# Eight floats of padding in front of the large SBUF tile of a hybrid decoder trunk

## The chip, the cores and the metric

The kernel runs on one core of one Trainium2 chip. The time is device microseconds of one execution, the median of several runs. The profile is one further execution, recorded by the hardware profiler; its times are given from the first instruction to the last (the span).

## What is computed

The reference is a decoder of four layers over 256 tokens of 1024 numbers, all in float32. Each layer is a token mixer (HGRN2, FoX attention, Mamba-2 SSD, HGRN2) followed by a PEER feed-forward part, and a final RMS norm ends it. The PEER part is what moves the data:

```python
def peer_ffn(h, w_q, sub_keys, u_tab, v_tab):
    ...
        q = (xb @ w_q).reshape(M, PEER_HEADS, 2, PEER_HALF)
        s = jnp.einsum('mhcd,hckd->mhck', q, sub_keys).astype(jnp.float32)
        sv, si = lax.top_k(s, PEER_TOPK)
        ...
        u = jnp.take(u_tab, idx, axis=0)
        v = jnp.take(v_tab, idx, axis=0)
        act = jax.nn.gelu(jnp.einsum('md,mhkd->mhk', xb, u).astype(jnp.float32), approximate=False) * gates
        return jnp.einsum('mhk,mhkd->md', act.astype(xb.dtype), v)
```

For each token, 8 heads choose 16 of 16384 experts each. Every chosen expert needs its own row of u and of v, 1024 floats each, which differ from token to token. That is 256 x 8 x 16 = 32768 row pairs for each layer, 8192 bytes a pair.

## The kernel before

**The eight stages.** A stage is one layer's PEER part for one half of the tokens. The halves are 128 tokens, but a gather serves 64 tokens twice over: 128 partitions hold two experts for each of 64 tokens. A stage is 64 pairs of gathers (8 heads by 8 positions q, and in each pair g = 0 and 1, the two groups of 64 tokens), so 512 pairs, 1024 gathers in all. The last pair is split into six smaller gathers, which makes 1028.

**One gather.** u and v stand side by side in one table, in_uv, with rows of 2048 floats. `gather` (line 1517) is an indirect DMA on POOL's queue: each of the 128 partitions gets one row of 8192 bytes, 1 MB for a gather. `fetches` issues them as long as the deque `ring` has a free buffer. The ring holds GB, seven buffers of 2 x 1024 floats for each partition, and now and then a spot that is free for a while.

**What is done with it.** `dot` multiplies the u half by the token's vector and sums it on VectorE (line 230 is the helper that all VectorE work goes through). `active` applies GELU on ScalarE and scales a 128x64 matrix dg with it (helper line 243). `spread` multiplies dg with the v half on TensorE into an accumulator (line 1587) and gives the buffer back to the ring.

**The work beside it.** While stage s runs, the mixer, the norms and the queries of stage s + 1 run piece by piece between the pairs; a cost estimate decides when the next piece is let in. Their weights come as units of 128 x 2048 floats, 1 MB, issued by `loads` (line 417) in a list's order, into one of these places: a raw buffer (pool raw, two of them), a kept spot (eight, plus one in mix), a home borrowed from another part of the arena. SP issues most of them; ScalarE (ACT) issues those that fill a kept spot in step with the projections, on a queue of its own. A few query units are parked as two halves in free columns of mix (line 415). The places come from PARK:

```python
PARK = {"hg": (6 * D, 7 * D), "fox": (6208, 7232), "ssd": (192, 192 + 3 * D + 96)}
```

**Where things lie.** The pool c has buffers of its own in the order in which its tiles are asked for: cst (784 floats for each partition), par (386), fst (192), the arena (49216), and then small tiles (eps, spare, rts, trimask, m64). Behind that pool lie the two raw buffers and the pool wk2 with dg, dots and the routing's small tiles. A tile's size is rounded up to 32 bytes. Below the pool lie 2048 bytes for each partition that hold DMA descriptors (SCRATCH), and four constants of 32 bytes each. So the arena begins at byte 2048 + 128 + 3136 + 1568 + 768 = 7648 of each partition, the first raw buffer at 205024. cst begins at 2176, par at 5312 and fst at 6880. The four dots buffers lie 32 bytes apart.

The arena is one tile that is cut by hand: h, xT, XR, keys, SS, mix, kept, gb. All these widths are multiples of 64 floats, so that every part starts as far past a multiple of 256 bytes as the arena does. Within mix, all places for loads do too, except the second of the SSD layer's parked halves at float 3360, which is 52 x 256 + 128 bytes into mix.

The change stands in `trunk`, which is the whole program; the lines that it moves stand below it by one.

Of the kernel before, what the change touches and what calls it, by code (L numbers as in the profile page):

```python
# [11 lines left out]
F32 = mybir.dt.float32  # L12
# [7 lines left out]
P = 128  # L20
# [170 lines left out]
def trunk(ctx: ExitStack, tc: tile.TileContext, d: dict, out: bass.AP):  # L191
    nc = tc.nc
    SB = bass.MemoryType.PSUM
    cpool = ctx.enter_context(tc.tile_pool(name="c", bufs=1))
# [11 lines left out]
    fst = cpool.tile([P, P + 8 * 2 * DEPTH], F32, name="fst")  # L206
    sizes = (("h", D), ("xT", D), ("XR", 2 * D), ("keys", UNIT), ("SS", 2048), ("mix", MIX), ("kept", NKEPT * UNIT),
             ("gb", NGB * 2 * D))
    arena = cpool.tile([P, sum(n for _, n in sizes)], F32, name="arena")
    at_, o_ = {}, 0  # L210
    for name, n in sizes:
# [1555 lines left out]
```

## Time and profile before

| | |
|---|---|
| time, median of 3 runs | 3123.55 us (3118.79 to 3123.78) |
| profiled execution: time, span | 3126.04 us, 3124.2 us |
| mean granted TensorE clock | 0.946 |
| moved by DMA | 1266.72 MB, mean 405 GB/s over the span |
| busy: TensorE, VectorE, ScalarE, POOL | 83%, 67%, 50%, 39% |

In the profile's rows, L230 is line 230 of the kernel, out<-in names the tiles that an instruction writes and reads, and x1028 counts instructions. The DMA section lists the queues with their packets, megabytes, and the time that the packets took as a share of 16 DMA engines over the span or the stretch asked for. A packet here is one contiguous piece for one partition, or a semaphore word of 4 bytes that reports an engine's part of a DMA as done. Shares can exceed 100% slightly, where packets overlap. With a stretch given, the same section tells of that stretch alone, and that is how the price of packets of one kind can be read.

A row of the table of stretches has the stretch, its length, the busy time of TensorE, weight loads, VectorE, ScalarE and POOL with the number of instructions, and at its end the granted clock, the DMA share and GB/s. A row of waits reads: who waited, for whom, us in total, times, longest.

### The profile page before, as it was taken

The page shows a single profiled execution, that of the slowest core. Times are in us where ns is not written, and L with a number is a line of the kernel's source. Part 1 is how long each engine was busy: PE and PEld are TensorE (multiplying, and loading weights), DVE is VectorE, ACT ScalarE, POOL GpSimd, SP SyncE. Part 2 cuts the span into 40 slices and gives each one's busy share as a digit, 9 for nine tenths or more (in the row PEclk, how much of TensorE's full clock was granted, in tenths as well). Part 3 has the DMA queues.
Part 4 walks back from the last instruction along what each step waited for, and adds up shares of the span by engine and source line. Part 5 has one row for each costly group of instructions (what it writes and reads, how often), then busy time and mean ns, then how long its engine had stood idle before and what let it go on. Part 6 is the DMA issues. An engine that isn't in the chain of part 4 may idle for free.

```text
span 3124.2 us, 34210 instructions
## 1 busy us (share of the span) xinstructions
PE 2595.8 (83%) x10106; PEld 1102.8 (35%) x10106; DVE 2103.1 (67%) x5583; ACT 1566.2 (50%) x4486; POOL 1230.2 (39%) x1036
## 2 busy tenths in 40 slices
PE   9899887887689996988878998878877899876666
PEld 4444342233234452333234542523322343521111
DVE  1677667665857767778476886677657677677754
ACT  3465434463445744577345784355444565443433
POOL 0234334443443444333343333343334443455454
PEclk9999989998999998999999999999989999999999
DMA  8799999999999999999998999999999999999998
GB/s 338 281 410 420 420 419 419 408 412 420 418 412 419 397 419 411 401 416 404 407 416 357 391 412 420 418 411 418 420 416 409 401 418 420 419 419 420 419 420 341
DMA packets 176184, 1266.72 MB, mean 405 GB/s; under 512 B 19585, under 2 KB 20225, under 8 KB 22913
## 3 DMA queue, kind: packets, MB, share of 16 engines
q0 software_dynamic: 147776, 1073.81, 83.8%
q1 hardware_dynamic: 24480, 163.47, 12.7%
q10 hardware_dynamic: 3744, 27.26, 2.1%
q8 instruction: 83, 1.36, 0.2%
q14 instruction: 101, 0.82, 0.1%
HBM read 1263.41 MB, written 1.05 MB: 405 GB/s over the span
## 4 chain that ended last, share of the span: by engine, by line
DMA 48%; PE 16%; issue 14%; DVE 13%; POOL 5%; ACT 4%; POOLq 0%; DVEq 0%; ACTq 0%
DMA arena<-in_uv,ix 46%; DVE arena L230 9%; PE pj L271 6%; PE acc L1587 5%; POOL arena L1517 5%; PE ps L271 4%; ACT L243 2%; DVE eq L230 1%; DMA raw<-in_ssm 1%; ACT dg L243 1%; PE ps L275 1%; ACT arena L243 1%; DVE af L230 1%; DVE gs L230 0%; DVE si L230 0%
## 5 line engine op out<-in xcount | busy, mean ns | idle before, releaser
L1517 POOL DMA_INDIRECT arena<-in_uv,ix x1028 | 1227.8, 1194 | 1877.8 <-PE acc L1587 1095.9
L230 DVE SCALAR_TENSOR_TENSOR arena<-arena 128x1024 f32<-128x1024 f32 (+2 forms) x1088 | 1266.1, 1172 | 815.8 <-DMA arena<-in_uv,ix 797.5
L1587 PE MATMUL acc<-arena,dg 128*64 128x512 f32 x4096 | 1396.9, 660 | 472.4 <-ACT dg L243 468.4
L243 ACT ACTIVATE dots<-dots 128x1 f32<-128x1 f32 x1024 | 203.1, 198 | 1239.6 <-DVE arena L230 1237.8
L1587 PEld LDWEIGHTS acc<-arena,dg 128*64 128x64 f32 x4096 | 344.0, 144 | 1338.5 <-ACT dg L243 941.2
L271 PE MATMUL pj<-arena 128*128 128x128 f32 (+1 forms) x1760 | 437.2, 401 | 2.1 <-DVE arena L230 1.2
L243 ACT ACT_TABLE_LOAD x331 | 424.7, 1283 | 6.9 <-PEq L1758 0.7
L243 ACT ACTIVATE dg<-dg,dots 128x64 f32<-128x64 f32 x1024 | 356.2, 348 | 33.2
L271 PE MATMUL pj<-raw,arena 128*128 128x512 f32 x736 | 351.5, 619 | 20.8 <-DMA raw<-in_ssm 16.5
L271 PEld LDWEIGHTS pj<-arena 128*128 128x128 f32 x1760 | 246.9, 192 | 189.4 <-issue 172.9
L243 ACT ACTIVATE dg<-m,gs 128x64 f32<-128x64 f32 x1024 | 294.0, 335 | 1.0
L271 PE MATMUL ps<-arena 128*128 128x128 f32 (+6 forms) x1664 | 229.0, 285 | 10.1 <-DMA arena<-in_wq 7.4
L271 PEld LDWEIGHTS ps<-arena 128*128 128x128 f32 (+3 forms) x1664 | 184.5, 177 | 109.9 <-issue 54.8
L271 PEld LDWEIGHTS pj<-raw,arena 128*128 128x128 f32 x736 | 134.5, 194 | 237.0 <-issue 203.7
L243 ACT ACTIVATE arena<-ps 128x256 f32<-128x256 f32 (+4 forms) x186 | 64.7, 391 | 45.9 <-PE ps L271 45.4
L230 DVE DVE_READ_ACCUMULATOR arena<-arena 128x1 f32 x1024 | 83.8, 82 | 0.0
L271 PE MATMUL ps<-cst,arena 128*128 128x128 f32 (+3 forms) x288 | 71.7, 368 | 0.0
L275 PEld LDWEIGHTS ps<-fst,arena 128*128 128x128 f32 x440 | 50.7, 144 | 57.8 <-issue 29.6
L275 PE MATMUL ps<-fst,arena 128*128 128x128 f32 x440 | 69.6, 285 | 1.2 <-DVE arena L230 0.6
L230 DVE FIND_INDEX8 si<-sv,arena 128x8 uint32<-128x128 f32 x256 | 69.7, 284 | 0.0
L230 DVE MAX8 sv<-arena 128x8 f32<-128x128 f32 x256 | 61.5, 282 | 4.0 <-ACT arena L243 4.0
L230 DVE SCALAR_TENSOR_TENSOR arena<-arena,cst 128x128 f32<-128x128 f32 x224 | 62.2, 345 | 0.3
(132 smaller groups left out, 1414.8 us busy)
## 6 DMA issues: line engine op xcount, KB each, us to landing
raw<-in_ssm SPq DMA_DIRECT2D x48, 1024.0 KB, 9.6
raw<-in_hg SPq DMA_DIRECT2D x30, 1024.0 KB, 9.1
arena<-in_hg SPq DMA_DIRECT2D x22, 1024.0 KB, 17.2
arena<-in_wq SPq DMA_DIRECT2D x21, 1024.0 KB, 9.7
arena<-in_uv,ix POOLq DMA_INDIRECT x1028, 13.6
raw<-in_fox SPq DMA_DIRECT2D x14, 1024.0 KB, 9.4
raw<-in_wq SPq DMA_DIRECT2D x9, 1024.0 KB, 9.1
arena<-in_fox ACTq DMA_DIRECT2D x9, 1024.0 KB, 9.4
```

What stands on the lines that cost most here:

```text
L230: return getattr(nc.vector, name)(o, *a, **k)
L243: nc.scalar.activation(o, i, f, **k)
L271: nc.tensor.matmul(o, w, m, start=start, stop=stop)
L275: nc.tensor.transpose(o, i, ident)
L1517: nc.gpsimd.indirect_dma_start(o, None, src, bass.IndirectOffsetOnAxis(ap=ix, axis=0))
L1587: nc.tensor.matmul(accs[s][e][g * 64:g * 64 + 64], dg[:, g], v, start=False, stop=hh == 7 and q == NQ - 1)
```

## The change

A tile of eight floats for each partition, 32 bytes, is asked for in front of the arena. Nothing writes or reads it. The arena then begins at byte 7680, and all tiles behind it lie 32 bytes further.

```diff
     fst = cpool.tile([P, P + 8 * 2 * DEPTH], F32, name="fst")
     sizes = (("h", D), ("xT", D), ("XR", 2 * D), ("keys", UNIT), ("SS", 2048), ("mix", MIX), ("kept", NKEPT * UNIT),
              ("gb", NGB * 2 * D))
+    cpool.tile([P, 8], F32, name="pad")
     arena = cpool.tile([P, sum(n for _, n in sizes)], F32, name="arena")
     at_, o_ = {}, 0
     for name, n in sizes:
```

## The prediction

> **What bounds the kernel now.** I read the page first: the span, the DMA rows, the queues and the chain of work that ended last.
>
> ```profile
> span 3124.2 us, 34210 instructions
> ...
> DMA  8799999999999999999998999999999999999998
> GB/s 338 281 410 420 420 419 419 408 412 420 418 412 419 397 419 411 401 416 404 407 416 357 391 412 420 418 411 418 420 416 409 401 418 420 419 419 420 419 420 341
> DMA packets 176184, 1266.72 MB, mean 405 GB/s; under 512 B 19585, under 2 KB 20225, under 8 KB 22913
> ## 3 DMA queue, kind: packets, MB, share of 16 engines
> q0 software_dynamic: 147776, 1073.81, 83.8%
> q1 hardware_dynamic: 24480, 163.47, 12.7%
> q10 hardware_dynamic: 3744, 27.26, 2.1%
> ...
> DMA 48%; PE 16%; issue 14%; DVE 13%; POOL 5%; ACT 4%; POOLq 0%; DVEq 0%; ACTq 0%
> ```
>
> The 16 DMA engines are busy nearly everywhere, and the rate has a ceiling: slice after slice stands at 418 to 420 GB/s. Queue q0 carries POOL's gathers, q1 SP's loads, q10 ACT's loads. The chain is a wait for DMA in 48% of its length. Then the stages (the table of stretches; DMA share and GB/s end each row) and the waits:
>
> ```profile
> 100.00:500.00 400.00, 347.07 (x1536) 162.18 (x1535) 282.88 (x799) 197.29 (x570) 159.06 (x136) 0.94 0.99 408
> ...
> 1300.00:1500.00 200.00, 175.48 (x648) 74.35 (x645) 161.09 (x433) 150.11 (x370) 75.76 (x61) 0.94 1.00 400
> ...
> 2500.00:3000.00 500.00, 393.10 (x1502) 153.94 (x1500) 357.41 (x946) 231.37 (x721) 233.06 (x189) 0.95 1.01 419
> 3000.00:3124.00 124.00, 81.77 (x205) 19.20 (x204) 61.07 (x105) 40.55 (x148) 55.67 (x43) 0.94 0.90 371
> ```
>
> ```profile
> POOL arena L1517 <- PE acc L1587: 1095.9, 392, 8.2
> ...
> DVE arena L230 <- DMA arena<-in_uv,ix: 797.5, 564, 4.6
> ```
>
> From 100 to 3000 us the DMA engines have no free time, and VectorE waits 797.5 us for gathered rows. POOL, which could issue earlier, waits for a free buffer (1095.9 us). So the packets set the pace: a cheaper packet shortens the kernel, and a packet of the same price leaves it alone. The question is what of a packet's price hangs on the address it is written to.
>
> **The change, part by part.** The pad tile is read and written by nothing: no instruction, no DMA, no wait and no semaphore is added or removed, and no queue's order changes. It takes 32 bytes of each partition, and everything allocated behind it moves by 32: the arena from byte 7648 (29 times 256, and 224) to 7680 (30 times 256), the two raw buffers from 205024 (also 224 past a multiple) to 205056, and the small tiles behind them. All gathers, unit loads and key loads now start 224 past a multiple of 256 and will start on one. Of all wide loads only one half of a parked unit in the SSD layer differs: 128 bytes further, so 96 past a multiple now and 128 past it afterwards.
>
> First, the price of a packet. A stretch in which q0 runs alone, and one in which SP loads 1024 bytes to each partition (the SSD layer's small weights, into par, start 192):
>
> ```profile
> DMA packets 5769, 42.01 MB, mean 420 GB/s; under 512 B 642, under 2 KB 642, under 8 KB 642
> ## 3 DMA queue, kind: packets, MB, share of 16 engines
> q0 software_dynamic: 5765, 41.97, 101.3%
> ```
>
> ```profile
> DMA packets 276, 1.13 MB, mean 416 GB/s; under 512 B 26, under 2 KB 154, under 8 KB 154
> ## 3 DMA queue, kind: packets, MB, share of 16 engines
> q0 software_dynamic: 138, 1.00, 89.4%
> q1 hardware_dynamic: 138, 0.13, 14.1%
> ```
>
> The first is 2900 to 3000 us: 101.3% of 16 x 100 us is 1620.8 us for 5765 packets and 41.97 MB; 642 of the packets are semaphore words. The second is 1182.88 to 1185.6 us: 14.1% of 16 x 2.72 us is 6.136 us for 138 packets, which are 128 of 1024 bytes (154 less 26) and 10 semaphore words, 0.131 MB. Two equations with a price per packet and a price per byte give 8.9 ns for each packet and 37.4 ns for each 1000 bytes (428 GB/s over 16 engines). A packet of 8192 bytes costs 306.3 + 8.9 = 315.2 ns. Rounding of the 14.1% moves the 8.9 by 0.2.
>
> The output stores, whose destination is the output in HBM, test the line (3121 to 3123.5 us):
>
> ```profile
> DMA packets 288, 0.52 MB, mean 210 GB/s; under 512 B 32, under 2 KB 32, under 8 KB 288
> ## 3 DMA queue, kind: packets, MB, share of 16 engines
> q1 hardware_dynamic: 288, 0.52, 56.6%
> ```
>
> The line gives 288 x 8.9 ns + 0.524 MB x 37.4 = 22.2 us; the row has 56.6% of 40 us, 22.6 us. So 8.9 ns is a toll on every packet, on 2048-byte stores to rows of 4096 bytes as on loads into SBUF at 192 and at 224, and a semaphore word of 4 bytes fits in with it. Over the run it is 176184 - 19585 = 156599 data packets x 8.9 ns / 16 = 87 us for each engine. That is the most that a start address could explain.
>
> Does the toll depend on the start? One pair in this trace answers, the parked halves of the SSD layer's first query unit (line 415): 128 packets of 4096 bytes each, same queue, two halves of the same rows, one behind the other, written at 224 (1539.3 to 1543.1 us) and at 96 past a multiple (1543.1 to 1546.8 us):
>
> ```profile
> DMA packets 289, 1.57 MB, mean 414 GB/s; under 512 B 33, under 2 KB 33, under 8 KB 161
> ## 3 DMA queue, kind: packets, MB, share of 16 engines
> q0 software_dynamic: 144, 1.05, 66.6%
> q1 hardware_dynamic: 145, 0.52, 34.3%
> ```
>
> ```profile
> DMA packets 284, 1.56 MB, mean 421 GB/s; under 512 B 30, under 2 KB 30, under 8 KB 158
> ## 3 DMA queue, kind: packets, MB, share of 16 engines
> q0 software_dynamic: 142, 1.03, 67.2%
> q1 hardware_dynamic: 142, 0.52, 35.4%
> ```
>
> At 224: 34.3% of 60.8 us is 20.85 us, less 17 semaphore words at 9 ns, over 128: 161.7 ns. At 96: 35.4% of 59.2 us is 20.96 us, less 14 words, over 128: 162.8 ns. If the toll were paid by the distance to the multiple below, the second would be 8.9 x (1 - 96/224) = 5.1 ns cheaper; it is 1.1 ns dearer, and 0.1% in a row is 0.5 ns. So between 96 and 224 the start costs nothing that shows.
>
> The trace has no wide load at a start of zero, so that price is bounded. From below: the whole toll goes, 87 us of engine time. From above: a packet as dear as in the dearest stage (third rival). I take no change, since the price stays level over the starts that are there and since 4-byte words pay it too. What would hide a cheaper packet is nothing; if the toll does go, the gain is real.
>
> [...]
>
> Second, the engines. Their operands in the arena, in raw and in the small tiles move by 32 bytes as well. The dots tile answers here: its four buffers lie 32 bytes apart, and the two activations of line 1570 and 1571 run over all four.
>
> ```profile
> L243 ACT ACTIVATE dots<-dots x1024: 185/203/212, 117.2 to 3115.2; 128x1 f32<-128x1 f32 x171
> L243 ACT ACTIVATE dg<-dg,dots x1024: 347/348/351, 117.5 to 3115.5; 128x64 f32<-128x64 f32 x171
> ```
>
> The second takes 347 to 351 ns wherever its scale lies, so a step of 32 bytes costs at most 4 ns on it: 1024 x 4 ns = 4 us either way if each sat on the chain, which has ACT at 4%, so 0.2 us. VectorE and TensorE have no such pair; bounded by the same 4 ns in 350 (1.1%) on their 13% and 16% of the chain it is 3124 x 0.29 x 1.1% = 10 us either way. I take zero, as the ACT rows do.
>
> Sum: 0 (pad) + 0 (packets) + 0 (engines). The profiled execution took 3126.04 us, its span of 3124.2 and 1.8 around it; the median of the runs is 3123.55, 2.5 lower. So a profiled execution stays at about 3126 and the median at 3123.5.
>
> **The rivals.** One: the toll is the price of not starting on a multiple of 256, whatever the distance, and goes away. For it: starts of 96, 192 and 224 are all alike to such a mechanism, so the pair above cannot refute it. Against it: a 4-byte semaphore word pays the same. Price: at most 87 us x 2900/3124 (the stretch with a share of 0.99 to 1.01) = 81 us; at least 48% of 87, the share of DMA in the chain, 42 us. I take 65, nearer the full stages, since PE at 175 of 200 us in the stretch from 1300 would hold some back: 3124 - 65 = 3059 in the span, 3058 for the median, and 3042 to 3082 as its own range. 21%.
>
> Two: the pad does not move the arena, because an unused tile is dropped or packed elsewhere. Nothing in the profile speaks for it; the time is that of the forecast, 3123.5. 3%.
>
> Three, slower: packets that begin on a multiple of 256 get in one another's or the engines' way in SBUF, with all rows of every buffer on the same phase. Its place is every gather; its price is that of the dearest stage, 1400 to 1500 us:
>
> ```profile
> DMA packets 5417, 39.50 MB, mean 395 GB/s; under 512 B 599, under 2 KB 599, under 8 KB 599
> ## 3 DMA queue, kind: packets, MB, share of 16 engines
> q0 software_dynamic: 4394, 32.04, 81.0%
> ```
>
> By the line q0 would need 32.04 x 37.4 + 4394 x 0.0089 = 1237 us there; it took 1296, 4.8% more, with packets that start at 224 like all others. Over the run it took 83.8% of 16 x 3124.2, 41889 us, against 41476 by the line, 1.0% more. It decides if the mean excess rises above that 1.0%. At 395 GB/s throughout the span is 3124 x 405/395 = 3203, the median 3202. Against it: that stage is dear at the old starts too, and 224 is as much one phase for all buffers as zero is. 5%.
>
> **How the numbers follow.** A change under 0.2% (6.2 us) can't be told from none; the runs before spread over 5.0 us. No change in the packets: 64%, and with the second rival 67% within 0.2%. The first rival gives 21% faster, the third 5% slower. The 10 us of the engines, split by their sign, give another 4% faster and 3% slower. So faster 25%, same 67%, slower 8%. The forecast's own range is 3113 to 3134 (the engines' bound of 10 us). To leave no more than 2 in 10 out it must reach into the first rival, past its middle: 3056 below, and 3136 above.
>
> **What would show it.** Right: from 2900 to 3000 us q0 alone again moves about 5765 packets at 419 to 420 GB/s, q0 holds 83.8% of the span, and the chain keeps DMA near half. Wrong by the first rival: the ceiling rises to about 432 GB/s (420 x 2530/2459, eight packets and a word with and without the toll on data) and the span falls by 40 to 80 us. Wrong by the third: the ceiling falls below 415 with more packets in flight than the line pays for. The parked halves will lie at 0 and at 128: if the first becomes cheaper than the second, the start matters after all.

## The result, and the profile after

The changed kernel takes 3073.53 us (median of 4 runs, 3071.72 to 3074.91) against 3123.66 us before: a ratio of 0.9842, with a 95% interval of 0.9825 to 0.9859. It is 1.6% faster. The forecast was no change at 67%; the time lies in its range, at the place of the first rival. One later execution of the same kernel took 7130.79 us, with TensorE's 128x512 matmuls into acc at 1747 ns in place of 658 for a cause that stays open, and the ratios below leave it out.

First the page of the changed kernel: the span, the DMA rows, the queues and the chain.

```profile
span 3073.1 us, 34210 instructions
...
DMA  8699999999999999999999999999999999999998
GB/s 344 277 416 424 427 426 427 420 424 427 420 425 423 404 422 419 404 422 400 413 425 370 400 414 427 426 413 427 427 426 424 420 417 426 426 427 427 427 427 349
DMA packets 176183, 1266.72 MB, mean 412 GB/s; under 512 B 19584, under 2 KB 20224, under 8 KB 22912
## 3 DMA queue, kind: packets, MB, share of 16 engines
q0 software_dynamic: 147776, 1073.81, 83.7%
q1 hardware_dynamic: 24480, 163.47, 12.8%
q10 hardware_dynamic: 3744, 27.26, 2.1%
...
DMA 48%; PE 15%; DVE 15%; issue 14%; POOL 5%; ACT 3%; POOLq 0%; DVEq 0%; ACTq 0%
```

Instructions and megabytes are the same, and so are the packets of the three data queues. The ceiling has moved, from 418 to 420 GB/s to 424 to 427. The three queues together held 98.6% of 16 engines in both runs: 3080.5 us of 3124.2 before and 3030.1 of 3073.1 now. So each DMA engine works about 50 us less for the same bytes (the shares are rounded to 0.1%, 3 us), and the span is 51 us shorter: all of it arrives at the end.

The waits and the stretch from 2900 to 3000 us, in which q0 runs alone, in the changed kernel:

```profile
DVE arena L231 <- DMA arena<-in_uv,ix: 744.7, 534, 5.0
```

```profile
DMA packets 5864, 42.72 MB, mean 427 GB/s; under 512 B 651, under 2 KB 651, under 8 KB 651
## 3 DMA queue, kind: packets, MB, share of 16 engines
q0 software_dynamic: 5860, 42.67, 101.1%
```

VectorE waits 53 us less for gathered rows. In the stretch, 101.1% of 1600 us less 651 semaphore words of 9 ns are shared by 5209 rows of 8192 bytes: 309.4 ns for each, where it was 315.2.

The stretch of the SSD layer's small weights (1164.9 to 1167.6 us; rows of 1024 bytes into par, whose address the pad doesn't move) and the scaling on ScalarE:

```profile
q0 software_dynamic: 138, 1.00, 87.6%
q1 hardware_dynamic: 138, 0.13, 13.8%
```

```profile
L244 ACT ACTIVATE dg<-dg,dots x1024: 347/348/351, 117.2 to 3064.4; 128x64 f32<-128x64 f32 x171
```

Here lies a hint that the experiments follow up: the 138 packets of q1 take 13.8% of 43.2 us, 5.96 us, where they took 6.14, although their own start is what it was. The engines' operands, 32 bytes further, cost nothing that shows: the scaling takes 347 to 351 ns as before, and VectorE is busy for 2100.8 us, where it was 2103.1.

### The profile page after: what moved, and what is told of

Its sections match the earlier page's. It is cut to its first block, busy times and chain, and to the rows that moved or that the text cites. A ratio compares the mean times of both kernels' runs of the same rounds, so it can differ in the third digit from the quotient of the medians.

```text
span 3073.1 us, 34210 instructions
## 1 busy us (share of the span) xinstructions
PE 2586.2 (84%) x10106; PEld 1099.6 (36%) x10106; DVE 2100.8 (68%) x5583; ACT 1566.1 (51%) x4486; POOL 1217.4 (40%) x1036
## 4 chain that ended last, share of the span: by engine, by line
DMA 48%; PE 15%; DVE 15%; issue 14%; POOL 5%; ACT 3%; POOLq 0%; DVEq 0%; ACTq 0%
DMA arena<-in_uv,ix 47%; DVE arena L231 10%; PE pj L272 6%; PE acc L1588 5%; POOL arena L1518 5%; PE ps L272 4%; ACT L244 1%; DVE eq L231 1%; ACT dg L244 1%; DMA raw<-in_ssm 1%; DVE af L231 1%; PE ps L276 1%; DVE si L231 0%; DVE gs L231 0%; DMA arena<-in_wq 0%
## 5 line engine op out<-in xcount | busy, mean ns | idle before, releaser
L1518 POOL DMA_INDIRECT arena<-in_uv,ix x1028 | 1215.0, 1182 | 1839.7 <-PE acc L1588 1077.6
L272 PE MATMUL pj<-raw,arena 128*128 128x512 f32 x736 | 345.3, 609 | 17.0 <-DMA raw<-in_ssm 14.3
```

Of the source, the lines that this page charges most:

```text
L272: nc.tensor.matmul(o, w, m, start=start, stop=stop)
L1518: nc.gpsimd.indirect_dma_start(o, None, src, bass.IndirectOffsetOnAxis(ap=ix, axis=0))
```

## The experiments

**Loads alone, start by start.** A kernel that holds nothing but loads of 1 MB, with this as its core (P is 128 partitions, W a row of 2048 floats, NB 20 buffers of PITCH 2112 floats, ROUNDS 3):

```diff
+CASES = [(0, 0), (8, 0), (16, 0), (24, 0), (32, 0), (40, 0), (48, 0), (56, 0), (0, 56), (56, 56), (0, 0)]
...
+    for to, frm in CASES:
+        for _ in range(ROUNDS):
+            for b in range(NB):
+                o = (n % 120) * P * W + frm
+                n += 1
+                nc.sync.dma_start(arena[:, b * PITCH + to:b * PITCH + to + W],
+                                  u[o:o + P * W].rearrange("(p w) -> p w", w=W))
```

> Loads alone: SP loads of 1 MB (128 rows of 8192 bytes), 60 one behind the other for each case, into places whose start lies 0, 32, 64, 96, 128, 160, 192, 224 bytes past a multiple of 256, then 0 with the source 224 past, 224 with the source 224 past, and 0 again. Everything the decoder computes is left out. Theory A (graded): the read side of a packet costs its bytes and a toll whatever the start; the write side loses what lies below the start, and shows only where it is the longer of the two. Then 0 to 64 stand at the floor of about 309 ns a packet of 8192 bytes, and the price rises from there by about 1.2 ns for every 32 bytes to about 315 ns at 224. Theory B (one more piece): every start off a multiple costs the same, 315 ns at 32 as at 224. Theory C (only 64 or 128 matter): 64 and 128, or 128 alone, are as cheap as 0 and the others cost 315 ns. Theory D (not the packets): all alike at one price, and the time came from engines whose operands moved. A source 224 past with the destination on a multiple: about 315 or more if reads lose what lies below their start, 309 if they don't.

The q1 rows of one stretch of 100 us from each case, in the order of the cases (packets, MB, share): destination at 0, 32, 64, 96, 128, 160, 192, 224; then destination 0 with the source at 224; both at 224; both at 0.

```profile
q1 hardware_dynamic: 5874, 42.76, 101.2%
...
q1 hardware_dynamic: 5771, 42.04, 101.2%
...
q1 hardware_dynamic: 5789, 42.18, 101.3%
...
q1 hardware_dynamic: 5792, 42.17, 101.4%
...
q1 hardware_dynamic: 5791, 42.16, 101.3%
...
q1 hardware_dynamic: 5789, 42.18, 101.4%
...
q1 hardware_dynamic: 5798, 42.21, 101.4%
...
q1 hardware_dynamic: 5777, 42.05, 101.3%
...
q1 hardware_dynamic: 5873, 42.76, 101.2%
...
q1 hardware_dynamic: 5768, 42.02, 101.3%
...
q1 hardware_dynamic: 5872, 42.74, 101.1%
```

A destination on a multiple of 256 bytes gets 428 GB/s, one at 32 or 224 gets 420, one from 64 to 192 gets 422. One ninth of each count is semaphore words (655 of 5874 at 0); worked out as above, a row takes 309.1 ns at 0, 314.4 at 32, 313.8 at 128 and 314.6 at 224. The graded theory falls, since 32 costs as much as 224; so does the one in which 64 or 128 is enough, and the one without packets. A source 224 bytes further costs nothing that shows: the ninth row is as good as the first, 428 GB/s in both. (The source's start is counted from the table's own, whose address no run shows.)

**Other pads in the whole kernel.** The pad alone is changed, as in

```diff
-    cpool.tile([P, 8], F32, name="pad")
+    cpool.tile([P, 64], F32, name="pad")
```

with 64, 40, 24 and 16 floats, for starts at 224, 128, 64 and 32.

> 64 floats of padding in place of 8: the same tile in front of the arena, but the arena is back at 224 past a multiple of 256. If the start of the destinations is the cause (A, B, C): 3123 us, as before the change. If it is the pad as such, or the absolute place in SBUF: 3073.

> 40 floats of padding: arena and raw start 128 past a multiple of 256. A (graded): about 3090, since three of the seven 32-byte steps of loss are gone and the rest of it is partly hidden under the read side. B (any start off a multiple costs the same): 3123. C (128 is as good as 256): 3073.

> 24 floats of padding: arena and raw start 64 past a multiple of 256. A (graded): 3073 to 3080, the loss of two steps hides under the read side. B: 3123. C: 3073 if 64 is enough, 3123 if it takes 128.

> 16 floats of padding: arena and raw start 32 past a multiple of 256. By the series of loads 32 costs as much as 224 (314.6 and 314.7 ns): 3118 on this chip, ratio 0.998 to 1.000. By the graded theory, which the first runs speak against: 3075. If engines' operands and not packets made the gain, 32 is unlike both and nothing follows.

> The changed kernel once more, beside the others on the same chip: ratio 0.982 to 0.986.

The times stand beside runs of the kernel before on the same chip (3119.03 us in the first batch, 3120.92 in the second):

| start | pad, floats | median us | ratio to before, 95% interval |
|---|---|---|---|
| 224 | 64 | 3118.46 | 0.9999 (0.9989 to 1.0009) |
| 128 | 40 | 3108.10 | 0.9964 (0.9950 to 0.9978) |
| 64 | 24 | 3111.29 | 0.9968 (0.9956 to 0.9981) |
| 32 | 16 | 3118.58 | 0.9992 (0.9983 to 1.0002) |
| 0 | 8 | 3072.77 | 0.9843 (0.9826 to 0.9859) |

A pad that brings the arena back to 224 is worth nothing (3118.46 us against 3119.03), so it is the start modulo 256 that counts, not the pad or the place. 64 and 128 gain a fifth of the way, 32 nothing, as in the loads alone (422, 422 and 420 GB/s, between 420 at 224 and 428 at 0). The graded theory had about 3090 for 128 and 3073 to 3080 for 64, so it falls here too; one more piece had the time of before for both, nearer, though they came out 8 and 11 us below it. Why the starts in between gain a little stays open. The q0 rows from 2850 to 2950 us, where gathers run alone, for the pads of 64, 40 and 8 floats (the last is the changed kernel):

```profile
q0 software_dynamic: 5761, 41.96, 101.2%
```

```profile
q0 software_dynamic: 5785, 42.13, 101.3%
```

```profile
q0 software_dynamic: 5853, 42.62, 101.0%
```

The gathers have nearly the rates of the plain loads: 420, 421 and 426 GB/s at 224, 128 and 0.

**Row sizes.** Loads alone, with rows of other widths and buffers far enough apart:

```diff
+CASES = [(2048, 2112, 0), (2032, 2112, 0), (2032, 2112, 16), (2032, 2112, 32), (512, 576, 0), (512, 576, 56),
+         (1024, 1088, 0), (1024, 1088, 56), (4096, 4160, 0), (4096, 4160, 56), (2048, 2112, 1)]
```

> Loads alone again (all of the decoder is left out), 60 MB for each case: rows of 8192 bytes at start 0; rows of 8128 bytes at start 0, 64 and 128; rows of 2048, 4096 and 16384 bytes each at start 0 and 224; rows of 8192 bytes at start 4. The first series showed every start from 32 to 224 at 313.7 to 314.7 ns against 309.0 at zero. Theory B1 (one more piece): a write is cut at multiples of 256 bytes and every piece has a price; a row off the multiple has one piece more. Then 8128 bytes at start 64 (64 + 8128 = 8192, 32 pieces) stay at their floor of 307 ns, at start 128 (33 pieces) they cost about 5 ns more; rows of 2048, 4096 and 16384 bytes each cost the same 5 ns more at 224, so 84 becomes 89, 159 becomes 164, and about 610 becomes 615. Theory B2 (the start itself): 8128 bytes at start 64 cost the 5 ns too, and the other sizes 5 ns each. Theory B3 (every 256 bytes are cut in two): the loss grows with the bytes, 1.3 ns at 2048 and 10 at 16384, and 8128 bytes at 64 pay nearly all of it.

The q1 rows of 100 us each: rows of 8128 bytes at start 0, 64 and 128, and then 2048 bytes at 0 and 224, 4096 at 0 and 224, 16384 at 0 and 224.

```profile
q1 hardware_dynamic: 5914, 42.74, 101.3%
...
q1 hardware_dynamic: 5920, 42.74, 101.3%
...
q1 hardware_dynamic: 5791, 41.87, 101.4%
...
q1 hardware_dynamic: 22227, 40.47, 105.3%
...
q1 hardware_dynamic: 21180, 38.57, 104.8%
...
q1 hardware_dynamic: 11535, 42.01, 102.6%
...
q1 hardware_dynamic: 11248, 40.96, 102.7%
...
q1 hardware_dynamic: 2964, 43.06, 100.5%
...
q1 hardware_dynamic: 2937, 42.80, 100.7%
```

The first three decide it. 8128 bytes from 64 end at 8192 and touch 32 pieces of 256 bytes, as they do from 0: both take 307.1 ns. From 128 they touch a 33rd, and take 313.8. So a start off the multiple was not dear in itself (nothing lost at 64); one piece more was (6.7 ns at 128). The other pairs lose 3.8 ns at 2048 bytes, 4.2 at 4096 and 5.0 at 16384 (84.1 to 87.9, 159.0 to 163.2, 610.7 to 615.7): nearly the same for each row, however long, so it is not that each 256 bytes are cut in two. For short rows that is a far larger share, 4.7% of the rate at 2048 bytes. 8192 bytes at start 4 gave 419 GB/s, near the 420 at 32.

**Part of the destinations.** The arena on a multiple, raw back at 224, by a second pad behind the pool's last tile:

```diff
     m64 = cpool.tile([P, 64], F32, name="m64")
+    cpool.tile([P, 56], F32, name="pad2")
```

> The pad of 8 floats in front of the arena, and 56 floats behind the pool's last tile, so that the arena starts on a multiple of 256 and the raw buffers at 224 past one, as before. 101 of the loads of 1 MB go to raw, 12928 of some 156600 data packets. If a packet pays for its own start: 12928 x 5.3 ns / 16 = 4.3 us are lost again, 3073 of the gain's 50 us staying for the most part, about 3074 to 3078. If one misaligned stream slows its neighbours: clearly more than 4 us are lost, 3085 or above. If the gain came from raw, not from the gathers: 3115 to 3119.

3073.61 us, ratio 0.9849 (0.9833 to 0.9866), against 0.9843 for the pad alone on the same chip. The gain is the arena's. The 4.3 us for the loads into raw are within the interval, so the time does not say whether they were lost. The traces do. From 1800 to 1900 us q1 carries loads into raw alone; its rows before the change, with both at 224, then with raw alone at 224, then with both on a multiple:

```profile
q1 hardware_dynamic: 1572, 11.44, 27.6%
```

```profile
q1 hardware_dynamic: 1626, 11.88, 28.1%
```

```profile
q1 hardware_dynamic: 1606, 11.72, 27.7%
```

Worked out as above, a row takes 315 ns, 309 ns and 309 ns (0.1% of the share is 1 ns). The loads at 224 were as cheap as those on a multiple once the gathers beside them were on one, so the 4.3 us were not lost. The next run asks by itself how far that goes.

**A mixture.** Loads alone, of which a part, evenly spread, starts at 224:

```diff
+CASES = [(0, 12), (1, 12), (3, 12), (6, 12), (9, 12), (12, 12)]
...
+            to = 56 if (i + 1) * off // of > i * off // of else 0
```

> Loads alone (all of the decoder is left out), SP loads of 1 MB with rows of 8192 bytes, 96 for each case: none, 1 in 12, 3 in 12, 6 in 12, 9 in 12 and all of them start 224 bytes past a multiple of 256, evenly mixed, the others on a multiple. With none the rate was 428 GB/s, with all 420. Theory E (each load pays for its own start): the rate falls in a straight line, 427.3 at 1 in 12, 426 at 3 in 12, 424 at half, 422 at 9 in 12. Theory F (two sides: reads set the floor, writes with 33 pieces are slower than that, writes with 32 pieces are faster, and a short stretch of slow ones is made good by those behind it): 427 to 428 at 1 in 12 and 3 in 12, then falling, 424 to 427 at half, and 420 with all.

The q1 rows of 180 us for none, 1, 3, 6 and 9 in 12, and of 170 us for all:

```profile
q1 hardware_dynamic: 10559, 76.94, 101.1%
...
q1 hardware_dynamic: 10564, 76.95, 101.1%
...
q1 hardware_dynamic: 10575, 76.95, 101.1%
...
q1 hardware_dynamic: 10524, 76.65, 101.2%
...
q1 hardware_dynamic: 10454, 76.14, 101.2%
...
q1 hardware_dynamic: 9812, 71.47, 101.3%
```

427.4, 427.5, 427.5, 425.8, 423.0 and 420.4 GB/s: nothing is lost up to a quarter, where the straight line would have given 425.7, and the rate falls from somewhere before the half. Each row's place on its engine (16 engines times the stretch, by the rows in it) is 306.7 ns, the same, the same, 307.8, 309.9 and 311.8. From the half on it rises by 2 ns with every quarter, which points back to about 304 ns with none: below the 306.7 that are there. The author's estimate, worked out from these six places alone, is two things of which the slower sets the pace: one of 306.7 ns that doesn't know the start, and one of some 304 ns for 32 pieces and 312 for 33, about 9.5 ns a piece by either, with room between them in which a few slow rows are made good. No run shows the two apart. Places counted the same way from the rows further up fit the second: at 224, rows of 2048, 4096, 8192 and 16384 bytes take 85.0, 160.0, 311.8 and 612.6 ns, which is 9.4 ns for each of their 9, 17, 33 and 65 pieces. That the one is the read side and the other the write side was argued, not shown by itself; that the source's start cost nothing (428 GB/s with it alone at 224) and the destination's did (420) fits it. The small weights (47.2 to 45.9 ns a row) and the loads into raw (315 to 309 ns) fit as well: they got cheaper when only their neighbours were on a multiple.

## Why the prediction was right in its range and wrong in its likeliest case

**The range.** That the time lies in it was no merit of the forecast. The prediction itself called anything past 0.2% a change, and 1.6% came; its lower end held because it had been stretched into the first rival to cover what the forecast might miss.

**What bounds the kernel.** Right, and more fully than the prediction used it: all of the 50 us that each DMA engine lost came off the span. The rival's discount for the stages where PE is busy, 65 of 81, was not needed.

**The price of a packet.** The two equations were worked out rightly and read wrongly. Solved for the changed kernel's rows (1617.6 us for 5860 packets and 42.67 MB, 5.96 us for 138 packets and 0.131 MB), they give 8.3 ns for each packet and 36.8 ns for each 1000 bytes, after 8.9 and 37.4. So the gain came for the most part out of what was booked as the price of the bytes: 306.3 to 301.2 ns for 8192 bytes. That booking was wrong, as the loads alone show. A straight line through their rows of 2048, 4096, 8192 and 16384 bytes gives 8.6 ns for each row and 36.7 ns for each 1000 bytes on a multiple, and 12.6 and 36.8 at 224. So the bytes cost the same at either start, and the loss is some 4 ns for each row. Of the toll at 224, then, about a third hangs on the start and the rest stays.

The prediction's line missed that because its two kinds of rows carried different parts of the loss. The rows of 1024 bytes went from 47.2 to 45.9 ns, 1.3 less, without a move of their own, and the gathers beside them went from 315.2 to 309.4. The difference, 4.5 ns over 7168 bytes, is the 0.6 ns by which the price of 1000 bytes came out too high. The line's test, the output stores, goes to HBM and not into SBUF. That the 87 us held as a bound was luck: they were the sum of a term of which most did not move.

**The parked pair.** This is the step that failed: from "between 96 and 224 the start costs nothing that shows" the prediction went on to a term of zero for the packets. They gave 50 us for each DMA engine. The reading was right, the conclusion from it was not. 4096 bytes from 224 touch 17 pieces, and from 96 they touch 17 as well, so the two halves differed in the distance and not in what costs. Besides, two thirds of the bytes in both stretches were gathers at 224. The prediction said itself that such a mechanism could not be refuted by the pair, and then gave it 21%.

Its last sign, the same halves afterwards, would have misled too. They now lie at 0 (1517.2 to 1520.95 us) and at 128 (1520.95 to 1524.7 us):

```profile
q1 hardware_dynamic: 144, 0.52, 34.2%
```

```profile
q1 hardware_dynamic: 148, 0.52, 34.2%
```

Less 16 and 20 semaphore words, both take 159 ns, so the first is no cheaper than the second, though the start matters. It is as in the mixture: few rows off the multiple, among neighbours on one, cost nothing that shows.

**The semaphore words.** They were counted against the first rival, since 4 bytes paid the toll too. They do, and go on to: the traces' records of 4 bytes take 9 ns before and after. They belong to the part that stayed.

**The engines and the pad.** Zero within the noise, as forecast: at 224 with a longer pad the time is that of before (ratio 0.9999), and the scaling on ScalarE took 347 to 351 ns before and after the change. The second rival (the pad moves nothing) and the third (a lower ceiling) are out.

**The first rival.** Its mechanism in the text, a price for not starting on a multiple whatever the distance, is what the runs showed (5.3 ns a row at 32, 5.5 at 224), but for the rows that end on the same piece (8128 bytes from 64, 307.1 ns as from 0). What it took to go away was the whole toll, and most of that stayed. Its size was 65 us, with 42 to 81 as its range; it was 51 in the span, and the ceiling rose to 427 GB/s in place of the 432 that it was to show. Its weight was too low because the level price over the starts that were there was taken for evidence about the one that was not.

## What to carry to other kernels

In this kernel, bound by its DMA engines, the cheap SBUF destinations were those where a row touched as few 256-byte pieces as it could (in the loads alone 309.1 ns in place of 314.6 for 8192 bytes, 307.1 in place of 313.8 for 8128). So the place to try in another one is a multiple of 256, when rows are multiples of 256 themselves. Eight floats of padding were worth 1.6% with rows of 8192 bytes, and shorter rows had more to gain (4.7% at 2048 in the loads alone); in the loads alone it was enough that three quarters of them were so placed (427.5 GB/s, where all had 427.4). And a price that is level over all cases in a trace says nothing of a case that the trace lacks, when all of them share the property in question.

## What the hardware showed that was not expected

A row's price did not rise with the distance of its start from the multiple: 32 bytes off cost 5.3 ns, 224 cost 5.5, and 64 to 192 some 4.6 to 4.9, in loads alone. The cause of that small difference at both ends stays open. Up to 3 loads in 12 off the multiple cost nothing (427.5 GB/s, with none 427.4). And a source 224 bytes further in HBM cost nothing that shows, with the destination on the multiple or off it (428 and 420 GB/s, as without).
